# Strassen-Winograd down projection: activations kept as token blocks, loads a pass ahead, the riding tile and one sum made in the gate/up stage

## The chip, the cores and the metric

The kernel runs on one core of one Trainium2 chip. A core has a matrix engine (TensorE, in the profile PE, with its weight loads as PEld), a vector engine (DVE), a scalar engine (ACT), a general engine (POOL) and a queue engine that issues most transfers (SP); transfers are carried by 16 DMA engines. The metric is the device time of one execution in microseconds (us).

## The reference, cut to what matters

One layer of a diffusion backbone over 2048 tokens of width 1024: a mixer (Fourier and retention heads), an output projection, then a SwiGLU feed-forward block with an inner width of 2816, both blocks closed by a post-norm.

```python
u  = modulate(layer_norm(x1), shift, scale)          # (2048, 1024)
h  = silu(u @ w_gate) * (u @ w_up)                   # (2048, 2816)
y  = (h @ w_down) * gate
out = layer_norm(ALPHA * x1 + y, ln2_g, ln2_b)       # (2048, 1024)
```

The inputs and the result are float32. The kernel gets near float32 accuracy with three float16 matmuls for each product: high by high, high by low and low by high halves (`mm3`, L151 to L154). The halves are made by ACT (high) and DVE (low).

## The kernel before, in words

The part that the change touches is the feed-forward block. Its three matrix products are made by Strassen-Winograd's scheme with 7 instead of 8 products, named A11, A12, S2, S1, S3, A22 and S4; S1 to S4 are products of sums of quarters. The tokens are cut in two halves (`sb` 0 and 1). A second level of the scheme is used in the down projection alone.

**Gate/up (925 to 1757 us).** A loop over 11 blocks j of the inner width. For each j SP loads raw weights for gate and for up (`w_raws`, L1080, two halves each into the tile `raw`), POOL forms their sums (L964 to L967), ACT and DVE split the seven results into float16 halves (L148, L149) in tiles of a ring of 12 buffers called `ws`, and PE makes 14 products of 12 matmuls with 512 columns (`prod`). The results go to `sg`; POOL adds the quarters (L1247 to L1249, L1255) and `h_out` (L1228) writes each of the seven outer operands to DRAM tiles `h_d`. Beside each j runs `down(i, c)` (L1139): it loads a piece of the down weights, multiplies it by the gate row (L1147), makes the inner sums on POOL (L1160 to L1163 and L1172 to L1175), splits them into a tile `wdo` with two buffers, and SP writes seven of them to DRAM tiles `wd_d` (five at L1168, two at L1157). The last, odd tile of the inner width (j = 10) is kept apart; its weights (`wl`) are made by `down_last`.

**Down, first part (1757 to 2070 us).** Ten passes: five outer products o (A11, A12, S2, S3, A22) times two token halves, each with its own seven inner products. A pass loads four quarters of h and the odd tile (`h_load`), makes the inner sums with POOL (L1394, L1398, and L1382 for the odd tile) and DVE (L1395, L1396), splits each operand into `ho` (ACT L1134, DVE L1135, three buffers), and PE multiplies: 234 matmuls of 256 columns a pass, four products having the odd tile "ride" with them. The copies `p`, `b_` and `c` (L1500 to L1511, L1443) combine the seven results, which DVE adds to 16 `state` tiles. The h tiles have one buffer, so a pass's loads wait until DVE and POOL are done with the pass before; `tc.issue_after(before)` sets where they stand on SP.

**Down, second part (to 2182 us).** The outer products S1 and S4 (`ONE`), as plain products of 512 columns; then the residual, the norm and the output.

What sets the order: a scheduler puts the instructions of each engine in one fixed order ahead of time, and every engine works through its own in that order. A tile with k buffers waits, when asked for the next time, until the use k turns back has ended. The names and lines that matter are `h_out`, `down`, `h_load`, `w_load`, `h_ops` and `outer`.

Of the kernel before, what the change touches and what calls it, by code (L numbers as in the profile page):

```python
# [15 lines left out]
P = 128  # L16
# [63 lines left out]
def layer_kernel(ctx: ExitStack, tc: tile.TileContext, a, out):  # L80
# [860 lines left out]
    ORDER = (A11, A12, S2, S1, S3, A22, S4)  # L941

# [184 lines left out]
    h_d = [[dram_tile([P, HJ, 2, 512], F16, "h") if o in ONE else dram_tile([P, HJ, 512], F32, "h") for o in range(7)] for _ in range(2)]  # L1127
    wd_d = [dram_tile([P, HJ, 2, 2, 256], F16, "wd") if o in ONE else dram_tile([P, HP, 2, 7, 2, P], F16, "wd") for o in range(7)]
# [8 lines left out]
    def down(i, c):  # L1137

        raws = []  # L1139
        for half in range(2):  # L1140
            raw = raw_tile((P, 2, 4, P))
            r0 = (2 * i + HJ * half) * P
# [10 lines left out]
        def op(o, x):  # L1153
            if o in ONE:
                w = mk(cq, [P, 2, 2, 2, P], F16, tag="wdo", bufs=2)
                split(w[:, :, 0], w[:, :, 1], x)
                Q.dma_start(wd_d[o][:, 2 * i : 2 * i + 2, c], w.rearrange("p k s y n -> p k s (y n)"))  # L1157
                return
# [9 lines left out]
            Q.dma_start(wd_d[o][:, i, c], w)  # L1168
# [10 lines left out]
    def down_last():  # L1179

        raws = []
        for half in range(2):
            raw = raw_tile()
            rv = raw.rearrange("p c n -> p (c n)")
            Q.dma_start(rv, wd_in[(HJ - 1 + HJ * half) * P : HJ * (half + 1) * P])
            G.tensor_tensor(rv, rv, gt2, ALU.mult)
            raws.append(raw)
        for o, t in enumerate(right(*raws)):
            if o in ONE:
                for c in range(2):  # L1190
                    dst = wd_d[o][:, HJ - 1, c].rearrange("p s (y n) -> p s y n", y=2)
                    Q.dma_start(dst, t.rearrange("p s (y c n) -> p c s y n", y=2, c=2)[:, c])
# [3 lines left out]
    def w_load(o, q):  # L1196

        if o == 0 and q in (3, 4):
            r = []
            for lo in range(0, HP, 2):  # L1200
                n = min(2, HP - lo)
                t = ws_tile((P, 2, 2, 2, P))
                Q.dma_start(t[:, :n], wd_d[o][:, lo : lo + n, :, q])
                r.extend(t[:, i] for i in range(n))
            return r
        t = mk(d1 if q < 3 else dq, [P, HP, 2, 2, P], F16, tag=f"wd{q}")
        Q.dma_start(t, wd_d[o][:, :, :, q])
        return [t[:, k] for k in range(HP)]

    def h_load(o, sb):  # L1210

        r = {}
        for qd in (0, 2, 3, 1):
            f, e = divmod(qd, 2)
            r[qd] = mk(d1, [P, HP, 256], tag=f"h{qd}")
            ins = Q.dma_start(r[qd], h_d[sb][o][:, e : 2 * HP : 2, f * 256 : (f + 1) * 256]).ins
        last = ws_tile((P, 512), F32)
        Q.dma_start(last, h_d[sb][o][:, HJ - 1])
        return r, last, ins
# [6 lines left out]
    for j in range(HJ):  # L1226
# [3 lines left out]
        def h_out(sb, o, src):  # L1230
            if o in ONE:
                ht = ws_tile() if j == HJ - 1 else mk(cq, [P, 2, 512], F16, tag="ht", bufs=1)
                half_split(ht, src)
                src = ht
            Q.dma_start(h_d[sb][o][:, j], src)
# [25 lines left out]
        for gu, src in enumerate((wg_in, wu_in)):  # L1261
# [12 lines left out]
            def done(sb, quad, src, ps):  # L1274
# [11 lines left out]
                else:  # L1286
                    c = mk(cq, [P, 512], tag="c", bufs=2)
# [29 lines left out]
            def product(o, sb, loose=False):  # L1317
# [12 lines left out]
                elif o == S3:  # L1330
                    keep(sb, "b", prod(w, o, sb, None, d["x"]))
                    done(sb, 3, d["b"], d["z"])
# [12 lines left out]
            elif j == HJ - 1 and gu == 1:  # L1345
                for sb in (0, 1):
                    for o in ORDER:
                        product(o, sb, True)
                    if sb == 0:
# [6 lines left out]
                        w_next.update((q, w_load(0, q)) for q in range(1, 5))  # L1356
# [20 lines left out]
    def h_ops(q, last):  # L1377

        lt = raw_tile((P, 2, 768), F16)
        with tc.high_priority():  # L1380
            half_split(lt[:, :, 0:512], last)
            G.tensor_tensor(last[:, 0:256], last[:, 0:256], last[:, 256:512], ALU.subtract)  # L1382
            half_split(lt[:, :, 512:768], last[:, 0:256])

        def op(src):
            t = mk(d1, [P, 2, HP, 256], F16, tag="ho", bufs=3)
# [3 lines left out]
        s1 = mk(d1, [P, HP, 256], tag="s1")  # L1390
        for i in range(7):
            with tc.high_priority():
                if i == 1:
                    G.tensor_tensor(s1, q[2], q[3], ALU.add)  # L1394
                    V.tensor_tensor(q[2], q[0], q[2], ALU.subtract)  # L1395
                    V.tensor_tensor(q[0], s1, q[0], ALU.subtract)  # L1396
                elif i == 2:
                    G.tensor_tensor(q[1], q[1], q[0], ALU.subtract)  # L1398
                t = op((q[0], q[1], q[0], q[2], q[3], s1, q[1])[i])
# [5 lines left out]
    def residual(sb, f, name, row, hf):  # L1405
        s_ = state(name, sb, f)
        xr = raw_tile((P, 2, 512))
        for i in range(2):
            t = sb * 8 + row * 4 + f * 2 + i
# [204 lines left out]
```

## Time and profile before

| what | value |
| --- | --- |
| time, median of 3 runs | 2194.0 us (2193.85 to 2196.17) |
| the profiled execution: its time, its span | 2195.93 us, 2194.1 us |
| granted TensorE clock over the span | 0.973 |
| PE busy, DVE busy, POOL busy | 94%, 68%, 39% |
| gate/up | 925 to 1757 us |
| ten passes of the down projection | 1757.35 to 2070.2 us |
| plain products, first matmul without inner scheme to last | to 2182.4 us |
| after the last matmul | 11.7 us |

A start in the profile is counted from the start of the span. A row of the timeline gives start and duration; a bracket gives how long the engine was idle before it and what ended that. A row of the groups gives busy us and mean ns of one instruction. "L1135" is the line that issued it, and where a helper issues for many callers, the tile names tell which one it is.

### The profile page before, as it was taken

What the parts mean: (1) busy time and instruction counts of PE and PEld (TensorE: products, weight loads), DVE (VectorE), ACT (ScalarE), POOL (GpSimd) and SP (SyncE); (2) the same over time, 40 slices, a digit from 0 to 9 for tenths busy, and PEclk for the clock granted to TensorE, in tenths of its full rate; (3) what the DMA queues carried; (4) which work ended last, traced back from release to release, by engine and by line L of the source; (5) the groups of instructions that cost most, each with busy time, mean ns of one, the idle gap of its engine ahead of it and who ended that gap; (6) DMA issues with size and microseconds to landing.
All of it is one profiled execution on the core that took longest, in us unless ns stands there. A gap on an engine that the chain in (4) does not pass through costs nothing. (4 is left out here: it accounts for less than half of the span.)

```text
span 2194.1 us, 31196 instructions
## 1 busy us (share of the span) xinstructions
PE 2051.6 (94%) x11678; PEld 1185.6 (54%) x11678; DVE 1487.7 (68%) x2731; ACT 803.5 (37%) x1442; POOL 845.6 (39%) x838
## 2 busy tenths in 40 slices
PE   6987999999999999889999999999999979898997
PEld 4545676567558444434444444444443458776743
DVE  7767584765688677876656665666556278878866
ACT  5634542332223244443343333333433233333222
POOL 3412321221221156656556655665565142222110
PEclk8998999999999999989999999999999989999999
DMA  9502321221142566614343334343434186779543
GB/s 285 175 4 77 106 80 49 78 61 47 55 119 90 194 209 218 207 66 154 126 144 133 118 129 150 126 136 130 139 116 156 55 266 189 214 213 278 200 146 128
DMA packets 308745, 305.20 MB, mean 139 GB/s; under 512 B 14753, under 2 KB 248049, under 8 KB 307441
## 3 DMA queue, kind: packets, MB, share of 16 engines
q1 hardware_dynamic: 301776, 287.08, 40.9%
q10 hardware_dynamic: 6816, 16.12, 2.0%
q8 instruction: 92, 1.51, 0.3%
q14 instruction: 61, 0.49, 0.1%
HBM read 200.25 MB, written 102.90 MB: 138 GB/s over the span
## 5 line engine op out<-in xcount | busy, mean ns | idle before, releaser
L152 PE MATMUL proj<-ws,uhi 128*128 128x512 f16 (+1 forms) x768 | 251.1, 327 | 2.1 <-ACT sg L751 1.0
L154 PE MATMUL proj<-ws,ulo 128*128 128x512 f16 (+1 forms) x768 | 250.8, 327 | 0.0
L153 PE MATMUL proj<-ws,uhi 128*128 128x512 f16 (+1 forms) x768 | 250.7, 326 | 0.0
L153 PEld LDWEIGHTS <-ws 128*128 128x128 f16 x1296 | 128.2, 99 | 175.9 <-issue 26.6
L152 PEld LDWEIGHTS <-ws 128*128 128x128 f16 x1296 | 128.4, 99 | 157.1 <-issue 9.4
L154 PEld LDWEIGHTS <-ws 128*128 128x128 f16 x1296 | 128.0, 99 | 156.4 <-issue 6.7
L149 DVE SCALAR_TENSOR_TENSOR ws<-raw,ws 128x512 f16<-128x512 f32 x186 | 156.1, 855 | 75.3 <-ACT ws L148 74.3
L148 ACT ACTIVATE ws<-raw 128x512 f16<-128x512 f32 x186 | 112.4, 624 | 124.3 <-DMA raw<-in_w_ffn_gate_dram 36.6
L152 PE MATMUL proj<-u2b,ws 128*128 128x512 f16 x340 | 128.8, 383 | 10.3 <-ACT b L1294 6.3
L152 PE MATMUL misc<-u2a,ws 128*128 128x512 f16 x344 | 131.6, 382 | 6.0 <-ACT p L1294 3.8
L153 PE MATMUL misc<-u2a,ws 128*128 128x512 f16 x344 | 131.8, 383 | 0.0
L154 PE MATMUL misc<-u2a,ws 128*128 128x512 f16 x344 | 131.7, 383 | 0.0
L154 PE MATMUL proj<-u2b,ws 128*128 128x512 f16 x340 | 130.2, 383 | 0.0
L153 PE MATMUL proj<-u2b,ws 128*128 128x512 f16 x340 | 130.1, 383 | 0.0
L1134 ACT CAST ho<-h 128x1280 f16<-128x1280 f32 x60 | 75.0, 1258 | 126.3 <-DMA h<-h 29.0
L149 DVE SCALAR_TENSOR_TENSOR wdo<-raw,wdo 128x256 f16<-128x256 f32 (+1 forms) x100 | 63.4, 655 | 84.8 <-ACT wdo L148 83.8
L167 POOL TENSOR_TENSOR rstd<-ve,mhalf 128x1 f32<-128x1 f32 x66 | 38.4, 590 | 200.8 <-DVE ve L165 177.9
L207 DVE SCALAR_TENSOR_TENSOR macc<-raw,sil,macc 128x128 f32<-128x128 f32 x308 | 109.2, 387 | 3.2
L1135 DVE TENSOR_TENSOR ho<-h,ho 128x1280 f16<-128x1280 f32 x60 | 104.2, 1743 | 9.7 <-ACT ho L1134 9.7
L149 DVE SCALAR_TENSOR_TENSOR wdo<-ws,wdo 128x512 f16<-128x512 f32 (+2 forms) x70 | 59.3, 868 | 75.8 <-ACT wdo L148 74.3
L154 PEld LDWEIGHTS <-ho 128*128 128x128 f16 x764 | 76.2, 100 | 51.1 <-DVE ho L1135 34.2
L152 PEld LDWEIGHTS <-uhi 128*128 128x128 f16 x768 | 75.8, 99 | 44.0 <-issue 2.5
(496 smaller groups left out, 5498.6 us busy)
## 6 DMA issues: line engine op xcount, KB each, us to landing
h<-h SPq DMA_DIRECT2D x40, 640.0 KB, 5.4
raw<-in_w_mod_dram SPq DMA_DIRECT2D x44, 512.0 KB, 4.1
wd<-wdo SPq DMA_DIRECT2D x50, 448.0 KB, 2.5
wd<-wd SPq DMA_DIRECT2D x33, 640.0 KB, 8.5
h<-sg SPq DMA_DIRECT2D x66, 256.0 KB, 2.6
raw<-in_w_ffn_gate_dram SPq DMA_DIRECT2D x22, 512.0 KB, 4.7
raw<-in_w_ffn_up_dram SPq DMA_DIRECT2D x22, 512.0 KB, 5.8
h<-hs SPq DMA_DIRECT2D x44, 256.0 KB, 2.0
```

Source lines behind the costliest of these rows:

```text
L148: S.activation(hi, raw, AF.Copy, scale=scale)
L149: V.scalar_tensor_tensor(lo, raw, scale, hi, ALU.mult, ALU.subtract)
L152: T.matmul(o, sh, mh, start=first, stop=False, skip_group_check=onto)
L153: T.matmul(o, sh, ml, start=False, stop=False, skip_group_check=onto)
L154: T.matmul(o, sl, mh, start=False, stop=last, skip_group_check=onto)
L167: pows.append(G.tensor_tensor(rstd, ve, mhalf[:, 0:n], ALU.pow).ins)
L207: V.scalar_tensor_tensor(acc, raw[:, k], sil[:, v, k : k + 1], acc, ALU.mult, ALU.add)
L1134: S.copy(dst[:, 0], src)
L1135: V.tensor_tensor(dst[:, 1], src, dst[:, 0], ALU.subtract)
```

## The change

**In gate/up.** `h_d` of the five outer operands is stored as four blocks of token quarters. The odd tile is now j = 0 instead of j = 10; its float16 halves (512 columns) and those of the difference of its two halves (256 columns) are made in `h_out` at j = 0 and stored in `hl_d`. This takes 20 tiles of the `ws` ring. For every other j a block of 256 columns is written; at the even ones (j = 2 to 10) `h_out` reads the block that was stored at the j before back into a tile `s1` (two buffers), POOL adds, and SP writes the sum in its place: the inner S1 operand. The down weights are written product by product, so a write has pieces of 512 bytes (896 x 256 elements) where it had 3584 (128 x 1792), and a load has 5 KB in one piece for each partition.

**In the down passes.** Two sets of h tiles, one for each token half; the loads of a pass are asked for at the start of the pass before. The weights of a product are loaded right after its last use. The order of the products becomes A11, A12, S2, S1, S3, S4, A22. S2, S3 and A22 are accumulated onto the PSUM bank of A11, S4 onto that of S1, and DVE adds the bank straight to the state after each product (`outer`); the copies `p`, `b_`, `c` go. POOL's sums go; DVE forms three differences a pass instead of two. `ho` gets four buffers. The residual of two of the state rows moves to the plain products (`row_part`), and for one ACT puts it into the bank.

```diff
-    h_d = [[... else dram_tile([P, HJ, 512], F32, "h") for o in range(7)] for _ in range(2)]
+    h_d = [[... else dram_tile([P, 4, HP, 256], F32, "h") for o in range(7)] for _ in range(2)]
+    hl_d = [[None if o in ONE else dram_tile([P, 2, 768], F16, "hl") for o in range(7)] for _ in range(2)]
...
-            Q.dma_start(wd_d[o][:, i, c], w)
+            Q.dma_start(wd_d[o][:, :, i, c], w)
...
+            elif j == 0:
+                ht = ws_tile()
+                half_split(ht, src)
+                Q.dma_start(hl_d[sb][o][:, :, 0:512], ht)
+                d = mk(cq, [P, 256], tag="s1", bufs=2)
+                G.tensor_tensor(d, src[:, 0:256], src[:, 256:512], ALU.subtract)
+                ht = ws_tile((P, 2, 256))
+                half_split(ht, d)
+                Q.dma_start(hl_d[sb][o][:, :, 512:768], ht)
+            else:
+                k, e = divmod(j - 1, 2)
+                Q.dma_start(h_d[sb][o][:, e, k], src[:, 0:256])
+                if e == 0:
+                    Q.dma_start(h_d[sb][o][:, 2, k], src[:, 256:512])
+                else:
+                    Q.dma_start(h_d[sb][o][:, 3, k], src[:, 256:512])
+                    t = mk(cq, [P, 256], tag="s1", bufs=2)
+                    Q.dma_start(t, h_d[sb][o][:, 2, k])
+                    G.tensor_tensor(t, t, src[:, 256:512], ALU.add)
+                    Q.dma_start(h_d[sb][o][:, 2, k], t)
...
-            t = mk(d1, [P, 2, HP, 256], F16, tag="ho", bufs=3)
+            t = mk(d1, [P, 2, HP, 256], F16, tag="ho", bufs=4)
...
-                if i == 1:
-                    G.tensor_tensor(s1, q[2], q[3], ALU.add)
-                    V.tensor_tensor(q[2], q[0], q[2], ALU.subtract)
-                    V.tensor_tensor(q[0], s1, q[0], ALU.subtract)
-                elif i == 2:
-                    G.tensor_tensor(q[1], q[1], q[0], ALU.subtract)
+                if i == S2:
+                    V.tensor_tensor(q[0], q[2], q[0], ALU.subtract)
+                elif i == S3:
+                    V.tensor_tensor(q[2], q[3], q[0], ALU.subtract)
+                elif i == S4:
+                    V.tensor_tensor(q[1], q[1], q[0], ALU.subtract)
...
+        h_next = h_load(*TWO[n])
...
+            onto = x if q in (S2, S3, A22) else z if q == S4 else None
+            ps = bank(ALL_BANKS, (P, 2, 256)) if onto is None else onto
...
+            if sb and o < 4:
+                w_next[q] = w_load(o + 1, q)
```

**POOL, from block j = 0 to block j = 1.** Before, the last two operations of `down(0, 0)` (L1161, L1163) stand there, then the sums of the gate weights of j = 1 (L964 to L967, first four) and those of its up weights:

```order
357 L1161 TENSOR_TENSOR ws_10253<-raw_10191,ws_10253 128x128
358 L964 TENSOR_TENSOR raw_10276<-raw_10276 128x512
359 L1163 TENSOR_TENSOR ws_10253<-raw_10191,ws_10253 128x128
360 L966 TENSOR_TENSOR raw_10276<-raw_10278,raw_10276 128x512
361 L965 TENSOR_TENSOR ws_10280<-raw_10278,raw_10276 128x512
362 L967 TENSOR_TENSOR raw_10278<-raw_10278,ws_10280 128x512
363 L964 TENSOR_TENSOR raw_10506<-raw_10506 128x512
364 L1147 TENSOR_TENSOR raw_10778<-raw_10778,gt_9767 128x512
```

The quarter sums of j = 0 (L1247) come five rows later. Now, in the changed kernel's own line numbers, the quarter sums (L1272 to L1274, L1280) and the differences of the odd tile (L1245) stand first, and `down(0, 0)` begins after them (L1163):

```order
344 L1272 TENSOR_TENSOR hs_10194<-sg_9780 128x512
345 L1273 TENSOR_TENSOR hs_10194<-sg_9780 128x512
346 L1274 TENSOR_TENSOR hs_10194<-hs_10194,sg_9780 128x512
347 L1280 TENSOR_TENSOR sg_9779<-sg_9779,hs_10153 128x512
348 L1245 TENSOR_TENSOR s_2071_10202<-hs_10194 128x256
349 L1245 TENSOR_TENSOR s_2075_10216<-hs_10194 128x256
350 L1280 TENSOR_TENSOR sg_9780<-sg_9780,hs_10194 128x512
351 L1245 TENSOR_TENSOR s_2078_10241<-sg_9779 128x256
352 L1245 TENSOR_TENSOR s_2082_10270<-sg_9780 128x256
353 L1163 TENSOR_TENSOR ws_10291<-raw_10280 128x128
354 L1165 TENSOR_TENSOR ws_10291<-raw_10280 128x128
```

What moved: `h_out` of j = 0, which waits for the results of the last products of up at j = 0, went ahead of `down(0, 0)` and of the sums of the next gate weights, whose first one comes 20 rows below L1163.

**SP at the same place.** Before, one write of h, then the seven writes of `down(0, 0)` with the load of the second half of the gate weights of j = 1 (L1080) among them:

```order
228 L1235 DMA h_1940_9741<-sg_1993_9769 128x512
229 L1168 DMA wd_1968_9755<-wdo_2045_10202 128x1792
230 L1168 DMA wd_1970_9756<-wdo_2047_10215 128x1792
231 L1168 DMA wd_1972_9757<-wdo_2049_10232 128x1792
232 L1168 DMA wd_1974_9758<-wdo_2051_10245 128x1792
233 L1168 DMA wd_1976_9759<-wdo_2053_10258 128x1792
234 L1157 DMA wd_1978_9760<-wdo_2054_10266 128x2x512
235 L1080 DMA raw_2059_10278<-in_w_ffn_gate_dram 128x8x128
```

Now the same eight follow 24 writes of the odd tile and of S1 and S4 of j = 0, of which the last three are shown:

```order
249 L1243 DMA hl_1980_9761<-ws_2081_10266 256x1x512
250 L1238 DMA h_1966_9754<-ht_2084_10276 128x1024
251 L1248 DMA hl_1980_9761<-ws_2083_10272 256x1x256
252 L1171 DMA wd_1988_9765<-wdo_2089_10296 896x1x256
253 L1171 DMA wd_1990_9766<-wdo_2091_10309 896x1x256
254 L1171 DMA wd_1992_9767<-wdo_2093_10326 896x1x256
255 L1171 DMA wd_1994_9768<-wdo_2095_10339 896x1x256
256 L1171 DMA wd_1996_9769<-wdo_2097_10352 896x1x256
257 L1160 DMA wd_1998_9770<-wdo_2098_10360 128x2x512
258 L1081 DMA raw_2103_10372<-in_w_ffn_gate_dram 128x8x128
```

What moved: the load of the second half of the gate weights stands behind everything that block j = 0 writes. On ACT and DVE the split halves of the odd tile likewise stand ahead of those of `wdo`: eleven low halves of 512 columns, seven of 256 and five additions for `sg` stand on DVE between the result of up's A22 (first token half) and the first low half of `wdo` that POOL's sums feed. On PE, 16 matmuls of the gate product A11 of j = 1 that stood between up's products now come after all of them; the order of the rest is the same there.

**SP in the first down pass.** Before, the h quarters of pass (A11, second token half) (L1216, `h0_2822` first) follow the last writes of h:

```order
547 L1235 DMA h_1958_9750<-hs_2796_16157 128x512
548 L1235 DMA h_1964_9753<-ws_2797_16162 128x1024
549 L1235 DMA h_1956_9749<-sg_2714_15603 128x512
550 L1216 DMA h0_2822_16482<-h_1954_9748 128x5x256
551 L1216 DMA h2_2823_16484<-h_1954_9748 128x5x256
```

Now they (L1219, `h0_2834` first) stand behind the last quarter of the pass after it (`h3_2859`, of A12) and behind the last three round trips of the inner S1 sum (read L1258, write L1260):

```order
759 L1219 DMA h3_2859_16823<-h_1942_9742 128x1280
760 L1238 DMA h_1966_9754<-ws_2833_16518 128x1024
761 L1258 DMA s1_2831_16493<-h_1958_9750 128x256
762 L1260 DMA h_1960_9751<-s1_2829_16483 128x256
763 L1561 DMA ws_3035_19401<-wd_1998_9770 128x1024
764 L1258 DMA s1_2832_16514<-h_1956_9749 128x256
765 L1260 DMA h_1958_9750<-s1_2831_16493 128x256
766 L1260 DMA h_1956_9749<-s1_2832_16514 128x256
767 L1219 DMA h0_2834_16527<-h_1954_9748 128x1280
768 L1219 DMA h1_2835_16529<-h_1954_9748 128x1280
```

What moved: loads of two passes ahead and the round trips went in front of the loads of the very next pass. On PE two matmuls of that next pass stand after the products A11, A12, S1 and S2 of the first pass and before its S3, S4 and A22.

More of the change, by code (lines that the diff above doesn't have):

```diff
@@ L941, in layer_kernel @@
     ORDER = (A11, A12, S2, S1, S3, A22, S4)
+    DOWN = (A11, A12, S2, S1, S3, S4, A22)
     def left(q, s, eng):
@@ L1196, in w_load @@
     def w_load(o, q):
-        if o == 0 and q in (3, 4):
+        n_ = DOWN.index(q)
+        if o == 0 and n_ in (3, 4):
             r = []
@@ L1355, in layer_kernel @@
                         wl = wl_load(0)
-                        w_next.update((q, w_load(0, q)) for q in range(1, 5))
+                        w_next.update((q, w_load(0, q)) for q in DOWN[1:5])
             else:
@@ L1451, in outer @@
         else:
-            V.tensor_tensor(st("21"), st("21"), c, ALU.add)
+            V.tensor_tensor(st(into), st(of), ps, ALU.add)
     def block_done(o, sb, f):
-        if o == A12:
-            residual(sb, f, "11", 0, 0)
-            for i in range(2):
-                moments(sb, f, i, "11", 0, 0)
-        elif o == S3:
-            residual(sb, f, "a", 0, 1)
-            residual(sb, f, "22", 1, 1)
-        elif o == A22:
-            residual(sb, f, "21", 1, 0)
-            for i in range(2):
-                moments(sb, f, i, "21", 0, 1)
@@ L1468, in layer_kernel @@
-    for o in range(5):
-        for sb in range(2):
-            if o == 0 and sb == 0:
-                w = w_next
-                hq, last, before = h_next
-                w.update((q, w_load(0, q)) for q in (5, 6))
-            else:
-                with tc.issue_after(before):
-                    if sb == 0:
-                        w = {0: w_load(o, 0)}
-                    hq, last, before = h_load(o, sb)
-                    if sb == 0:
-                        wl = wl_load(o)
-                        w.update((q, w_load(o, q)) for q in range(1, 7))
-            if o == 0 and sb == 1:
+        if o == S3:
+            residual(sb, f, "22", 1, 1, "21")
@@ new lines, in row_part @@
+    def row_part(sb, name, row):
+        for f in range(2):
+            residual(sb, f, name, row, 0)
+            for i in range(2):
+                moments(sb, f, i, name, 0, row)
+    TWO = [(o, sb) for o in range(5) for sb in range(2)]
+    w = w_next
+    for o, sb in TWO:
+        hq, lt = h_next
+        n = TWO.index((o, sb)) + 1
+        if n < len(TWO):
+            h_next = h_load(*TWO[n])
+        if sb == 0:
+            if o == 0:
+                w.update((q, w_load(0, q)) for q in DOWN[5:])
@@ L1520, in layer_kernel @@
+        if sb:
+            w, wl = w_next, wl_next
+    slots = [(d1, f"h{n}", 1) for n in range(4)] + [(d1, "ho", 4)] * 4 + [(dq, f"h{n}", 1) for n in range(4)]
     turns = [0]
```

171 lines of the change are left out of this document (86 added, 85 removed).

## The prediction

> **What bounds the kernel now.** I read the page first, then the stretches of the down projection, then what PE and POOL wait for there, and last the timeline around the places where the order moves. The page's first lines:
>
> ```profile
> span 2194.1 us, 31196 instructions
> PE 2051.6 (94%) x11678; PEld 1185.6 (54%) x11678; DVE 1487.7 (68%) x2731; ACT 803.5 (37%) x1442; POOL 845.6 (39%) x838
> ```
>
> PE is busy 94%, so whatever the change can gain lies in the places where PE stands. Stretches, with us, then busy us of PE, PEld, DVE, ACT and POOL, granted clock, DMA share and GB/s; the first 38 us of the down projection, the rest of its ten passes, the plain products; and 100 us of gate/up:
>
> ```profile
> 1757.35:1795.13 37.78, 23.85 (x178) 17.90 (x177) 35.40 (x26) 12.67 (x15) 21.25 (x9) 0.89 0.98 304
> 1795.13:2070.20 275.07, 248.95 (x2183) 215.66 (x2184) 233.20 (x221) 93.61 (x95) 64.28 (x25) 0.97 0.72 220
> 2070.20:2182.40 112.20, 112.20 (x522) 50.88 (x520) 67.91 (x148) 22.36 (x30) 10.45 (x15) 1.00 0.43 141
> 1450.00:1550.00 100.00, 100.00 (x465) 45.32 (x464) 62.71 (x78) 37.08 (x73) 63.76 (x61) 1.00 0.41 139
> ```
>
> In gate/up and in the plain products PE never stands; it stands in the passes alone. Who waits there, from 1740 to 2060 us (engine, tile, line, releaser: us, times, longest):
>
> ```profile
> POOL s L1394 <- DMA h<-h: 85.3, 8, 16.9
> POOL h L1398 <- DVE ho L1135: 76.3, 9, 13.9
> PEld L154 <- DVE ho L1135: 34.2, 16, 4.5
> ACT ho L1134 <- DMA h<-h: 29.0, 6, 7.5
> ```
>
> It is one chain: h lands late because its one buffer comes free late, POOL's sum waits for h, DVE's difference for POOL, the split for that, PE for the split. One such stop in the timeline:
>
> ```profile
> 1861.28 0.27 PE L154 MATMUL tq<-wd,ho 128*128 128x256 f16 x1
> ...
> 1861.72 0.27 PE L153 MATMUL zt<-wd,ho 128*128 128x256 f16 x1
> 1865.69 0.39 PE L154 MATMUL zt<-wd,ho 128*128 128x256 f16 x1 [3.69 <-DVE ho L1135]
> 1865.87 0.42 PE L152 MATMUL zt<-wd,ho 128*128 128x256 f16 x1
> 1866.09 0.42 PE L153 MATMUL zt<-wd,ho 128*128 128x256 f16 x1
> ```
>
> Matmuls start every 0.11 us (four steps in 0.44), PE stands for 3.7, and then the starts are 0.2 apart, at about half rate.
>
> **The change part by part.** The sum is made against the profiled execution: 2195.93 us, span 2194.1. The median of the runs shown is 1.9 lower, 2194.0; I add the terms to that.
>
> *Passes after the first.* The 2183 matmuls of the second stretch at 0.11 us need 240 us, so of its 275 us 35 are lost, standing or at half rate. This bounds the gain. Is the cover there? DVE has, in a pass, seven splits, three differences and seven additions of a bank:
>
> ```profile
> L1135 DVE TENSOR_TENSOR ho<-h,ho 128x1280 f16<-128x1280 f32 x50 | 86.9, 1742 | 6.8 <-ACT ho L1134 6.8
> L1135 DVE TENSOR_TENSOR ho<-s,ho 128x1280 f16<-128x1280 f32 x8 | 11.9, 1487 | 0.8 <-ACT ho L1134 0.8
> L1395 DVE TENSOR_TENSOR h<-h,h 128x1280 f32<-128x1280 f32 x9 | 13.4, 1487 | 20.3 <-POOL s L1394 20.3
> L1443 DVE TENSOR_TENSOR c<-b,misc 128x512 f32<-128x512 f32 x4 | 2.7, 681 | 1.1 <-PE misc L154 1.1
> ```
>
> That is 10 x 1.49 + 7 x 0.68 = 19.7 us (21.4 if the splits stay at 1.74) against 234 x 0.11 = 25.7 on PE. DVE is no longer the bound, POOL is out, and the loads are asked for a whole pass earlier. I take 31 of the 35; the range is 22 (a few stops stay where DVE's residual and the next pass's splits meet) to 35. Term: **-31**.
>
> *From block j = 0 to j = 1 in gate/up.* This is the largest added term. Rows of before, in time:
>
> ```profile
> 971.43 0.46 POOL L1160 TENSOR_TENSOR ws<-raw 128x128 f32<-128x128 f32 x1 [6.33 <-PE misc L154]
> 975.18 15.92 SPq L1168 DMA_DIRECT2D wd<-wdo  x5
> 992.76 0.62 SPq L1080 DMA_DIRECT2D raw<-in_w_ffn_gate_dram  x1
> 997.52 0.63 ACT L148 ACTIVATE ws<-raw 128x512 f16<-128x512 f32 x1 [2.60 <-DMA raw<-in_w_ffn_gate_dram]
> 1002.64 0.38 PE L152 MATMUL misc<-u2a,ws 128*128 128x512 f16 x1
> 1006.09 0.38 PE L152 MATMUL misc<-u2a,ws 128*128 128x512 f16 x1
> 1015.59 0.38 PE L152 MATMUL tq<-u2b,ws 128*128 128x512 f16 x1
> ```
>
> POOL begins `down(0, 0)` at 971.43; its first write goes out at 975.18, the second half of the gate weights of j = 1 is asked for at 992.76 (17.6 us later), is there at 997.52 (4.8), and PE first uses it at 1015.59 (A12, bank tq): 18 us to spare. In the new order `down(0, 0)` comes behind `h_out` of j = 0, which waits for up's results. PE has the 16 matmuls of the next A11 (3.45 us) behind up now, so up's A22, first half, which ended at 1006.09, ends at about 1002.6, and its addition about 1003.3. From there DVE has 23 operations before the first low half of `wdo`: eleven of 512 columns, seven of 256, five additions. The nearest rows, of the same forms:
>
> ```profile
> L1135 DVE TENSOR_TENSOR ht<-hs,ht 128x512 f16<-128x512 f32 x20 | 27.7, 1384 | 3.2 <-ACT ht L1134 3.0
> L149 DVE SCALAR_TENSOR_TENSOR wdo<-ws,wdo 128x256 f16<-128x256 f32 x10 | 5.6, 556 | 38.5 <-ACT wdo L148 38.5
> L1289 DVE SCALAR_TENSOR_TENSOR sg<-c,sg 128x512 f32<-128x512 f32 x65 | 62.7, 968 | 1.0
> ```
>
> 11 x 1.38 + 7 x 0.56 + 5 x 0.97 = 24 us: the first write of `down(0, 0)` goes out at about 1027. The same 17.6 and 4.8 us later, and 1.3 for the two halves of the split, A12 could start at 1051. PE, which used to start it at 1015.59, stands in two parts (before A11 and after it), together **+35**. From below: POOL has done its sums by then, and the seven writes may go out in 10 us: +27. From above: each write of the ring waits 1 us longer and DVE stands for the tiles: +43. Two stops just behind it, where PE waited for ACT, go, since ACT has long caught up:
>
> ```profile
> 1025.63 0.56 PE L152 MATMUL misc<-u2a,ws 128*128 128x512 f16 x1 [2.11 <-ACT p L1294]
> 1036.09 0.38 PE L152 MATMUL proj<-u2b,ws 128*128 128x512 f16 x1 [0.84 <-ACT a L1294]
> ```
>
> Term: **-3** (0 to -3).
>
> *First down pass.* The odd tile's splits go, so its early stops shrink; but the h quarters of the next pass stand on SP behind a quarter of the pass after it, which waits for the split of A22 and that for S2's `ho` buffer. PE can do 132 matmuls of the pass and 12 of up's S4 (132 x 0.11 + 12 x 0.22 = 17 us, with 4 of early stops to 1778), then stands. The chain from there:
>
> ```profile
> L1134 ACT CAST ho<-h 128x1280 f16<-128x1280 f32 x51 | 63.8, 1258 | 110.6 <-DMA h<-h 23.2 <-PE misc L154 21.5 <-PE s L154 18.0
> h<-h SPq DMA_DIRECT2D x36, 640.0 KB, 4.7
> h<-sg SPq DMA_DIRECT2D x63, 256.0 KB, 2.6
> 1795.13 0.39 PE L154 MATMUL zt<-wd,ho 128*128 128x256 f16 x1 [3.64 <-DVE ho L1135]
> ```
>
> Split of A22 1.26 + 1.49, a write of the S1 round trips 2.6, its last read 2.6, POOL's addition and the issues some 2, the h quarter 4.7, its split 2.75: 17.4, so PE goes on at about 1796 with 132 done. Before, it went on at 1795.13 with 191 done (A11, A12, S2, S1, S3 and 29 of the next pass): 59 x 0.11 = 6.5 and the 1 us between, **+8** (0 to +13, since the round trips may be over before).
>
> *Gate/up otherwise.* A write of `wd` has pieces of 512 bytes now. The nearest rows: writes in 3584-byte pieces, and gate loads whose rows are 512 bytes.
>
> ```profile
> wd<-wdo SPq DMA_DIRECT2D x50, 448.0 KB, 2.5
> raw<-in_w_ffn_gate_dram SPq DMA_DIRECT2D x20, 512.0 KB, 4.5
> 1673.66 0.38 PE L152 MATMUL proj<-u2b,ws 128*128 128x512 f16 x1 [2.91 <-ACT b L1294]
> ```
>
> At the rate of the loads 448 KB take 3.9 us, 1.4 more; through the ring of two that is 4 us more for each j. In the middle blocks 18 us of slack hide it; at j = 9 to 10 PE waits already (2.91 at 1673.66), so it counts once: **+4** (0 to +10). The Trainium skill, "DMA: Bandwidth & Descriptors", section Specifications, says that transfers run at line rate from 512 bytes up; by that this term would be nothing, and the sum 4 us lower. The rows above speak for a price (114 KB per us in short rows against 179), though a load and a write may differ. The S1 round trips: ten reads and ten more writes at each even j, 2.6 us each, two tiles at a time, some 26 of 72 us; a POOL addition behind a read holds what is behind it on POOL, a late tile holds SP. **+2** (0 to +5).
>
> *Plain products and the end.* PE is full there and DVE has 44 of 112 us free; the moved residuals fit. After the last matmul the same chain of work stands as before. 0 (-3 to +3).
>
> Sum: -31 + 35 - 3 + 8 + 4 + 2 = +15, so 2194 + 15 = **2209 us**.
>
> **The rivals.** *The stop at j = 1 is small* (the faster side). With POOL quiet, DVE's operations of 512 columns take 0.68 (as L1443 above) instead of 1.38, those of 256 some 0.4, and 23 of them 11 x 0.68 + 7 x 0.4 + 5 x 0.68 = 14 us; the writes of `down(0, 0)` start at 1017, go out in 10 us, since POOL has everything ready, and A12 starts 6.1 us later, at 1033. The term is +18 and the time 2192; with the first pass also at nothing it is 2184. It decides where the two terms together fall under 20. For it: PE's long stop leaves DMA and DVE free. Against it: the order is fixed, POOL works on the odd tile's differences in just these 24 us, and the 17.6 us of before came through the ring of two that is still there. Chance 0.26.
>
> *The bank becomes the wait.* S2, S3, A22 and S4 may not start before DVE has read the bank they add to. If DVE's addition stands behind a split that itself waits for PE, each of four products a pass waits for 0.7 and more: 36 products after the first pass, some 0.6 us each, 20 us of the 31 are gone again and the time is 2229. Against it: there is a product of 3.3 to 4 us between a bank's reading and its next use, and DVE has 6 us free a pass. Chance 0.12.
>
> *The change doesn't shorten the passes at all*, since transfers bound them (DMA share 0.72, and 0.98 in the first stretch): loads a pass ahead just queue. 2209 + 25 = 2234. Against it: 220 GB/s where the first stretch has 304, and the same bytes. Chance 0.06.
>
> **How the numbers follow.** The forecast has the remaining 0.56; its own range is 2198 to 2220, from the bounds of the first two terms (nine and eight either way, not all at once). To hold 8 in 10 I reach down to 2182 over most of the first rival and up to 2226. A measurement of this kernel tells about 0.2%, 4.4 us, from no change. Faster by more: the first rival where the passes also give their full 35 or the first pass costs nothing, and the forecast's lower edge, 0.25; within: 0.08; slower: 0.67.
>
> **What would show it.** Right: in the changed profile PE stands twice between 1005 and 1055 us, before bank tq of j = 1, with ACT or DVE `ws` as releaser, 35 us in all; POOL's L1163 starts behind the quarter sums; PE stands some 15 us in the first pass; and from then PE is busy over 98% at a clock near 1.0 until the end. The first term is wrong if PE still waits for `ho` in most passes; the second if A12 of j = 1 starts before 1035; the third if no stop over 8 us lies before 1800.

## The result, and the profile after

The changed kernel takes 2248.0 us (median of 4 runs, 2244.1 to 2252.2) against 2193.9 for the kernel before, measured beside it: slower, by a ratio of 1.0245 (1.0225 to 1.0265). The forecast, 2209 with a range from 2182 to 2226, had the sign and not the size.

The first lines of the page after: PE's busy us are those of before (2053.0 and 2051.6), its share fell from 94% to 91%. Nothing was added to PE's work; it stands longer.

```profile
span 2245.4 us, 31485 instructions
PE 2053.0 (91%) x11678; PEld 1184.5 (53%) x11678; DVE 1458.8 (65%) x2697; ACT 804.1 (36%) x1440; POOL 826.9 (37%) x868
```

The stretches (us, then busy us of PE, PEld, DVE, ACT, POOL, granted clock, DMA share, GB/s). Gate/up from 1060 on in the kernel before:

```profile
1060.00:1757.35 697.35, 685.89 (x3150) 309.04 (x3147) 397.27 (x498) 250.96 (x494) 386.38 (x377) 0.99 0.38 128
```

The same after, then the first 42 us of the down projection, the rest of the ten passes and the plain products:

```profile
1060.00:1835.66 775.66, 731.81 (x3322) 326.35 (x3321) 434.40 (x534) 271.44 (x535) 459.21 (x457) 0.99 0.46 139
1835.66:1877.50 41.84, 21.56 (x144) 15.61 (x144) 23.02 (x19) 11.09 (x13) 13.10 (x9) 0.77 0.84 306
1877.50:2120.90 243.40, 243.19 (x2209) 217.00 (x2210) 183.63 (x163) 80.89 (x69) 0.00 (x0) 0.99 0.70 238
2120.90:2234.30 113.40, 113.40 (x528) 51.47 (x526) 75.45 (x157) 27.05 (x38) 12.12 (x15) 1.00 0.48 159
```

The third line after is what the change was made for: PE is busy in 243.19 of 243.40 us, where before it was in 248.95 of 275.07. The first line after is what undoes it: in gate/up from 1060 on PE now stands for 44 us (775.66 less 731.81), where it had stood for 11, and that is without the two long stops, which lie earlier.

Followed along the trace, the two profiled executions part as follows (span 2194.1 to 2245.4, +51.3):

| point in the trace | before | after | later by |
| --- | --- | --- | --- |
| A12 of the gate weights, block j = 1 (bank tq) | 1015.59 | 1058.84 | 43.3 |
| last matmul of gate/up | 1764.27 | 1844.35 | 80.1 |
| last matmul of the ten passes | 2070.10 | 2120.90 | 50.8 |
| last matmul | 2182.44 | 2234.33 | 51.9 |

Of the 43.3, 3.9 were there before the end of up at j = 0: up's last matmul starts 0.4 later, at 1014.05, and the 16 matmuls of A11 (3.45 us), which stood ahead of it before, are still to come. Why up itself runs later was not followed. So: 39.4 at the start of block 1, 36.8 in the rest of gate/up, 29.3 back in the passes.

What PE waits for from 1000 to 1835 us (engine, bank, line, releaser: us, times, longest): the two stops that the prediction spoke of, and below them many small ones behind ACT's copies `b` and `p`, which in the kernel before came to 8.3 and 4.9 us.

```profile
PE proj L152 <- ACT ws L148: 26.2, 1, 26.2
PE proj L152 <- ACT b L1319: 16.7, 10, 4.5
PE tq L152 <- ACT ws L148: 10.1, 1, 10.1
PE misc L152 <- ACT b L1319: 7.1, 3, 3.8
PE misc L152 <- ACT p L1319: 6.0, 7, 0.9
```

**The start of block 1**, in the timeline: POOL begins `down(0, 0)` (L1163), the five writes start on SP, the second half of the gate weights is asked for (L1081), is there when ACT splits it, and PE makes A12.

```profile
1027.60 0.63 POOL L1163 TENSOR_TENSOR ws<-raw 128x128 f32<-128x128 f32 x1
1033.99 17.71 SPq L1171 DMA_DIRECT2D wd<-wdo  x5
1040.62 0.61 PE L152 MATMUL proj<-u2b,ws 128*128 128x512 f16 x1 [26.19 <-ACT ws L148]
1053.70 0.65 SPq L1081 DMA_DIRECT2D raw<-in_w_ffn_gate_dram  x1
1058.16 0.63 ACT L148 ACTIVATE ws<-raw 128x512 f16<-128x512 f32 x1 [3.02 <-DMA raw<-in_w_ffn_gate_dram]
1058.84 0.61 PE L152 MATMUL tq<-u2b,ws 128*128 128x512 f16 x1 [10.06 <-ACT ws L148]
```

It is the chain of the prediction, link for link: first write, 19.7 us to the load (17.6 said), 4.5 to its landing, then A12. The first write stands 7 us later than the 1027 said: up itself ran 3.9 late, so that DVE's operations ended 3 us late, at 1030.2, and POOL, which only began its sums at 1027.60, made it 4 more. Behind the stops the matmuls take 0.61 to 0.63 instead of 0.38; the granted clock is 0.50 from 1040.62 to 1046.14 and 0.96 in the 2.7 us after that.

**Blocks 2 to 10.** After each block in which the round trips are made, this comes at the start of the next one (here j = 7). The rows in time: SP asks for a stored S1 block back; POOL first does the next `down` (L1150), for which it waited; then the addition; only then may DVE write `sg` again (L1306), ACT use that and copy `a`, and PE go on.

```profile
1533.61 0.38 SPq L1258 DMA_DIRECT2D s<-h  x1
1535.26 1.27 POOL L1150 TENSOR_TENSOR raw<-raw,gt 128x512 f32<-128x512 f32 x1 [3.00 <-DMA raw<-in_w_ffn_down_dram]
1536.49 0.73 POOL L1259 TENSOR_TENSOR s<-s,sg 128x256 f32<-128x256 f32 x1
1537.25 0.69 DVE L1306 TENSOR_TENSOR sg<-p,tq 128x512 f32<-128x512 f32 x1 [4.44 <-POOL s L1259]
1537.97 0.63 ACT L1307 ACTIVATE sg<-sg 128x512 f32<-128x512 f32 x1 [0.76 <-DVE sg L1306]
1538.50 0.57 ACT L1319 COPY a<-proj 128x512 f32<-128x512 f32 x1
1539.12 0.38 PE L152 MATMUL proj<-u2b,ws 128*128 128x512 f16 x1 [1.89 <-ACT a L1319]
```

`sg` holds the result that POOL's addition reads, so the next block's first result has to wait until that addition has run. What holds the addition is either of two things: its read, which by estimate, with the 2.6 us that such reads take in this trace (the median), lands at about 1536.2, and L1150 ahead of it, which waits 3.00 us for a load of its own and is done at 1536.53. No run separates them. DVE and ACT then stay late for the rest of the block, and PE stops again and again behind their copies.

**First pass.** PE stands for 15.4 us. The rows in time: the read back of an S1 block on SP, POOL's addition that waits for it (7 us after the read was asked for), ACT's first copy to a `state` tile, which goes right behind that addition, and PE, whose bank that copy had to read first. The last row is a second stop, behind the split of the next pass's h.

```profile
1860.82 0.44 SPq L1258 DMA_DIRECT2D s<-h  x1
1867.85 0.72 POOL L1259 TENSOR_TENSOR s<-s,hs 128x256 f32<-128x256 f32 x1 [1.91 <-DMA s<-h]
1868.61 0.58 ACT L1469 COPY state<-proj 128x512 f32<-128x512 f32 x1 [10.28 <-POOL s L1259]
1869.24 0.37 PE L152 MATMUL proj<-wd,ho 128*128 128x256 f16 x1 [15.39 <-ACT state L1469]
1877.62 0.28 PE L152 MATMUL s<-wd,ho 128*128 128x256 f16 x1 [3.43 <-ACT ho L1137]
```

### The profile page after: what moved, and what is told of

Its sections match the earlier page's. It is cut to its first block, busy times and chain, and to the rows that moved or that the text cites. A ratio compares the mean times of both kernels' runs of the same rounds, so it can differ in the third digit from the quotient of the medians.

```text
span 2245.4 us, 31485 instructions
## 1 busy us (share of the span) xinstructions
PE 2053.0 (91%) x11678; PEld 1184.5 (53%) x11678; DVE 1458.8 (65%) x2697; ACT 804.1 (36%) x1440; POOL 826.9 (37%) x868
## 4 chain that ended last, share of the span: by engine, by line
PE 39%; DVE 23%; DMA 15%; POOL 13%; ACT 5%; issue 4%; SPq 2%; POOLq 0%; DVEq 0%; ACTq 0%
PE proj L152 6%; PE proj L154 6%; PE proj L153 6%; DVE macc L207 3%; DVE ws L149 3%; DMA raw<-in_w_ffn_down_dram 2%; DMA wd<-wdo 2%; DMA raw<-in_w_ffn_gate_dram 2%; DVE wdo L149 2%; PE s L152 2%; PE s L153 2%; PE s L154 2%; PE misc L153 2%; PE misc L152 2%; DVE sg L1314 2%
## 5 line engine op out<-in xcount | busy, mean ns | idle before, releaser
L152 PE MATMUL proj<-u2b,ws 128*128 128x512 f16 x340 | 131.4, 388 | 53.8 <-ACT ws L148 26.2
L1137 ACT CAST ho<-h 128x1280 f16<-128x1280 f32 x70 | 87.6, 1258 | 175.1 <-DVE h L1415 39.4
L154 PE MATMUL proj<-u2b,ws 128*128 128x512 f16 x340 | 132.2, 389 | 0.0
L153 PE MATMUL proj<-u2b,ws 128*128 128x512 f16 x340 | 132.1, 389 | 0.0
L152 PEld LDWEIGHTS <-uhi 128*128 128x128 f16 x768 | 75.7, 99 | 43.9 <-issue 2.2
L153 PEld LDWEIGHTS <-uhi 128*128 128x128 f16 x768 | 75.4, 98 | 44.1 <-issue 2.6
L154 PEld LDWEIGHTS <-ulo 128*128 128x128 f16 x768 | 75.4, 98 | 42.9 <-issue 0.2
```

The lines of the kernel that those rows point to most:

```text
L152: T.matmul(o, sh, mh, start=first, stop=False, skip_group_check=onto)
L153: T.matmul(o, sh, ml, start=False, stop=False, skip_group_check=onto)
L154: T.matmul(o, sl, mh, start=False, stop=last, skip_group_check=onto)
L1137: S.copy(dst[:, 0], src)
```

## The experiments

The theory was that two causes cost the time, each by itself: the odd tile's work at j = 0, which puts `down(0, 0)` and the next weights behind it, and the S1 round trips, which hold `sg`. Rivals: the small pieces of the writes of `wd`; SP, on whose queue the round trips stand; and passes that only look better because something else moved. All ratios are to the kernel before, measured beside the run; "no addition" and "down first, sum in the passes" ran on another chip than the rest of the experiments. Stages are from the profiled execution: the last matmul of gate/up, and the ten passes from the first matmul of the down projection to the last of 256 columns. Each is one execution: the kernel before and the one with the new `wd` alone have equal times, and their passes differ by 5 us, so smaller differences in these columns say little.

| kernel | median us | ratio (95%) | gate/up ends | ten passes |
| --- | --- | --- | --- | --- |
| before | 2193.9 | 1 | 1764.3 | 312.8 |
| changed kernel | 2248.0 | 1.0245 (1.0225 to 1.0265) | 1844.4 | 285.2 |
| sum made in the passes | 2193.4 | 1.0008 (0.9999 to 1.0018) | 1800.5 | 276.8 |
| odd tile raw | 2207.7 | 1.0074 (1.0056 to 1.0091) | 1799.8 | 288.8 |
| both | 2153.6 | 0.9834 (0.9819 to 0.9848) | 1760.5 | 274.0 |
| down(0, 0) first | 2217.4 | 1.0125 (1.0110 to 1.0140) | 1817.8 | 286.4 |
| down first, sum in the passes | 2170.4 | 0.9904 (0.9886 to 0.9922) | 1775.2 | 275.8 |
| no read back | 2210.0 | 1.0093 (1.0077 to 1.0109) | 1816.2 | 278.7 |
| no addition | 2206.7 | 1.0079 (1.0064 to 1.0094) | 1819.6 | 270.2 |
| round trips on POOL's queue | 2248.3 | 1.0275 (1.0256 to 1.0294) | 1842.7 | 284.7 |
| before, with the new `wd` alone | 2189.6 | 0.9998 (0.9990 to 1.0007) | 1763.2 | 307.6 |
| both, one set of h tiles | 2170.4 | 0.9913 (0.9898 to 0.9928) | 1761.2 | 295.1 |

### The S1 sum made in the passes again

```diff
-                    t = mk(cq, [P, 256], tag="s1", bufs=2)
-                    Q.dma_start(t, h_d[sb][o][:, 2, k])
-                    G.tensor_tensor(t, t, src[:, 256:512], ALU.add)
-                    Q.dma_start(h_d[sb][o][:, 2, k], t)
...
+                if i == A11:
+                    G.tensor_tensor(q[2], q[2], q[3], ALU.add)
```

> The inner S1 sum goes back to POOL in the down passes (one addition of 1280 columns a pass), so the even blocks read nothing back and write no sum; the rest is the changed kernel. Theory 1 (the round trips hold SP's queue in the odd blocks, and what stands behind them comes late): the stops of blocks 2 to 10 fall back to those of before, some 30 us less, and the first down pass loses its 15 us stop: 2248 becomes 2205 to 2218, and the passes stay without a stop, since the addition is hidden by loads that are a pass ahead. Theory 2 (the 512-byte pieces of the weight writes make gate/up slow): 2248 less the first pass's 15, so 2230 to 2240, and the stops of the odd blocks stay.

2193.4 us, more gained than either theory had. Gate/up ends 43.9 earlier than in the changed kernel, 2 of them there before A12 of block 1 starts; from there to the end of gate/up it takes 743.7 us instead of 785.5. The passes take 8.4 less, and the stop behind `state` is gone. The two stops at block 1 are still there (26.2 and 9.8). What PE waits for from 1060 to 1760:

```profile
PE proj L152 <- ACT b L1315: 7.5, 3, 4.6
PE misc L152 <- ACT b L1315: 3.3, 2, 2.5
PE misc L152 <- ACT p L1315: 1.4, 2, 0.8
```

12.2 us, where the changed kernel has 40.2 in the same window and the kernel before 12.5.

### The odd tile stored raw and split in the down projection again

```diff
-                ht = ws_tile()
-                half_split(ht, src)
-                Q.dma_start(hl_d[sb][o][:, :, 0:512], ht)
...
+                Q.dma_start(hl_d[sb][o], src)
...
```

The splits and POOL's difference of the odd tile stand in `h_ops` of each pass again.

> The odd tile stays at j = 0 but is stored as it comes, in float32, and split in the down passes as before; the S1 round trips stay. Theory 1 (the 20 ws tiles of the split halves put the down weights of j = 0 and the next gate weights behind up's results): the two stops between 1010 and 1060 us go, 36 to 40 us less, 2208 to 2214. Rival (the halves cost engine time wherever they are made): what is gained at j = 1 comes back in the passes, where DVE then has 21 us of 25.6, at over 10 us: 2220 or more.

2207.7 us, just under what was expected. A12 of block 1 starts at 1017.5, and no stop is over 2.4 us there: without the odd tile's work in front the two stops do not come. The passes take 3.6 more than in the changed kernel, but with the sum also in the passes the raw tile makes them 2.8 shorter, so neither shows a price of its splits there.

### Both edits

> Both edits: S1's inner sum on POOL in the down passes, the odd tile stored in float32. Theory 1: the two gains add, 2248 - 40 - 35 = 2173, within 2162 to 2182, clearly faster than the kernel before (2194), since nothing but the passes' gain of some 30 us is left. Theory 2 (short pieces of the weight writes): 2190 to 2205.

2153.6 us: 1.7% faster than the kernel before, and faster than expected. Gate/up from 1060 and the passes after the first:

```profile
1060.00:1753.53 693.53, 684.26 (x3158) 309.17 (x3157) 402.07 (x500) 253.12 (x495) 392.10 (x377) 1.00 0.42 130
1790.00:2027.57 237.57, 237.57 (x2174) 212.56 (x2173) 202.96 (x177) 85.96 (x81) 37.07 (x15) 1.00 0.70 242
```

Gate/up ends about where it did before (1760.5 and 1764.3), and in the passes after the first PE never stands, though POOL works 37.07 us there. The four medians of one chip add up: before 2191.5; both edits 37.8 below it; the odd tile's work alone 39.8 above that (2193.4); the round trips alone 54.1 above it (2207.7). -37.8 + 39.8 + 54.1 = +56.1, and the change, measured apart from these four, is at +54.1. To some 2 us the two causes do not overlap, and together they are the whole loss.

### `down(0, 0)` ahead of up's products at j = 0

```diff
+            if j == 0 and gu == 1:
+                down(0, 0)
...
-        if j < 2 * HP:
+        if 0 < j < 2 * HP:
```

> The changed kernel with one call moved: the down weights of j = 0 are asked for ahead of up's products instead of behind them, so that their tiles of the ring come before those of the odd tile. No work is added or left out. Theory 1 (it is the place, not the work): the 36 us of the two stops shrink to under 8 us: 2208 to 2220. Rival (ACT's, DVE's and POOL's work for the odd tile itself makes the gate weights late): at most 15 us less, 2233 or more.

2217.4 us, within what theory 1 expected, but the stops did not shrink to under 8 us: one of 14.2 is left. The last of the odd tile's splits on ACT, the first split of the waiting weights, and PE:

```profile
1025.31 0.41 ACT L1137 CAST ws<-s 128x256 f16<-128x256 f32 x1
1025.62 1.15 ACT L148 ACTIVATE ws<-raw 128x512 f16<-128x512 f32 x2
1026.30 0.61 PE L152 MATMUL proj<-u2b,ws 128*128 128x512 f16 x1 [14.23 <-ACT ws L148]
```

The weights are there, but their split stands on ACT behind the last split of the odd tile. So the load behind `down(0, 0)`'s writes makes the larger part of the loss, and the splits standing in front make the rest. The same edit together with the sum in the passes:

> The changed kernel with the down weights of j = 0 asked for ahead of up's products and with S1's inner sum on POOL in the down passes: the odd tile's halves stay in gate/up. Theory 1 (place of the down weights and round trips are the two costs, independent of each other): 2248 - 31 - 55 = 2162, within 2155 to 2170, a little slower than with the tile stored in float32 (2153.6). Rival (the odd tile's halves in gate/up save work in the passes that the other version pays): 2150 or less.

2170.4 us, just over the upper edge. The stop is again 14.2. By the ratios the kernel is 15 us above that of both edits, by the medians 19; and of the first pair, the edit took 28 of the 40. So of the 40 us at block 1 some 12 to 19 are the odd tile's own work in front of the weights' splits, and the rest, the larger part, is the place of `down(0, 0)`. Giving the odd tile tiles outside the `ws` ring was not tried.

### The round trips taken apart

Without the read back (POOL adds the two halves of the tile at hand):

```diff
-                    Q.dma_start(t, h_d[sb][o][:, 2, k])
-                    G.tensor_tensor(t, t, src[:, 256:512], ALU.add)
+                    G.tensor_tensor(t, src[:, 0:256], src[:, 256:512], ALU.add)
```

> The changed kernel without the reading back: POOL adds the two halves of the block at hand instead, so the inner S1 operand is another sum (left out: the true S1 sum), while POOL's addition, both writes and the tile s1 stay. Theory 1a (the read is what holds SP: it waits for the write of the block that it reads and for a free s1 tile, and its 2 us stand before each addition): 2248 less 25 or more, under 2223, near the kernel without round trips (2193). Theory 1b (the number of instructions on SP and the second write weigh): less than 12 us gained, 2236 or more.

Without the addition (what was read is written again):

```diff
-                    G.tensor_tensor(t, t, src[:, 256:512], ALU.add)
```

> The changed kernel with the round trips kept (read, tile s1, second write), but without POOL's addition between them (left out: the inner S1 sum, the block goes back as it was read). Theory A (POOL stands: the addition waits for the read, and the sums of the next weights stand behind it): as fast as without the read, 2205 to 2218. Theory B (SP stands: the read waits for a write and a free tile, the second write waits for the read, and other transfers stand behind them): 2235 or more.

2210.0 and 2206.7 us: 20 and 17 above the kernel before on their chips, where the change is 54 above it: either half taken away gives 34 to 37 us of the 52 that both give. Both times are where theory 1a and theory A had them, but not for their reasons. The next section is about SP; and PE's waits are behind ACT's copies, not behind the sums of the next weights.

From A12 of block 1 to the end of gate/up, 785.5 us in the changed kernel and 743.7 with both halves taken away, the two take 761.0 and 762.8. A read without an addition or an addition without a read thus still costs 17 to 19 there, and what these are was not followed. The other 23 to 25 need both: an addition that comes late while it holds `sg`. Without the read, the order puts the last additions of a block right behind POOL's quarter sums or close to it, and DVE hardly waits for them. DVE's waits from 1060 to 1760, first of the changed kernel, then without the read back (where lines stand one lower):

```profile
DVE sg L1306 <- POOL s L1259: 23.7, 8, 4.7
```

```profile
DVE sg L1305 <- POOL s L1258: 5.0, 4, 1.3
```

The first pass points the same way. PE's stop behind ACT's copy to `state` is 15.4 us in the changed kernel and 14.0 with the raw odd tile, where both halves are there; with the addition alone, and with the read alone:

```profile
1829.10 0.37 PE L152 MATMUL proj<-wd,ho 128*128 128x256 f16 x1 [3.95 <-ACT state L1468]
```

```profile
1835.29 0.37 PE L152 MATMUL proj<-wd,ho 128*128 128x256 f16 x1 [6.59 <-ACT state L1468]
```

With neither it is absent. Why `state` waits for POOL at all is read from the code, not shown by a run: its tiles lie in space that the gate/up stage frees only when its last tiles, the round trips' among them, are done.

### The round trips on another queue

```diff
-                    Q.dma_start(t, h_d[sb][o][:, 2, k])
+                    G.dma_start(t, h_d[sb][o][:, 2, k])
...
-                    Q.dma_start(h_d[sb][o][:, 2, k], t)
+                    G.dma_start(h_d[sb][o][:, 2, k], t)
```

> The changed kernel with the read and the second write of the round trips issued by POOL instead of SP; no work is left out. Theory 1 (SP's fixed order: loads and writes behind a waiting round trip come late): gate/up loses most of its stops in the odd blocks, 15 to 40 us less, 2208 to 2233. Rival (the round trips hold POOL, whose addition waits for the read, and with it the sums of the next weights): no gain or a loss, 2243 or more.

2248.3 us, ratio 1.0275 (1.0256 to 1.0294): nothing gained. In the changed kernel SP waits in these places (1060 to 1760):

```profile
SPq L1258 <- DMA h<-s: 28.8, 20, 3.4
SPq L1258 <- DMA h<-sg: 16.0, 9, 2.6
SPq L1260 <- POOL s L1259: 14.8, 19, 1.7
```

With SP freed of them, POOL waits instead, ahead of its own work:

```profile
POOL s L1258 <- DMA h<-sg: 10.9, 4, 7.8
POOL s L1258 <- DMA h<-s: 10.1, 6, 3.9
```

SP's 60 us of waiting look like the cause, but the run without the addition speaks against it: SP waits 66 us at the read and the second write there, and gate/up is 23 us shorter all the same. On either of the two queues that were tried an engine in fixed order has to wait for the round trip. One thing stays open: DVE's wait for POOL at `sg`, 23.7 us in the changed kernel, is only 2.9 here, and nothing is gained by it. With POOL issuing the round trips the time goes elsewhere, and where was not followed.

### The layout of the down weights alone, in the kernel before

```diff
-    wd_d = [... else dram_tile([P, HP, 2, 7, 2, P], F16, "wd") for o in range(7)]
+    wd_d = [... else dram_tile([P, 7, HP, 2, 2, P], F16, "wd") for o in range(7)]
...
-            Q.dma_start(wd_d[o][:, i, c], w)
+            Q.dma_start(wd_d[o][:, :, i, c], w)
```

> The kernel before with one thing of the change: the layout of the down weights (writes in 512-byte pieces, loads of 5 KB in one piece). Theory 1 (the S1 round trips slow the odd blocks, not these pieces): no more than 0.2% from before, the five writes of a block take 16 us as before. Theory 2 (short pieces cost a price in gate/up): 4 to 25 us slower.

Ratio 0.9998 (0.9990 to 1.0007): in the kernel's time the pieces of 512 bytes cost nothing. The five writes at a middle block, of the kernel before and of this run, take the same time through the ring:

```profile
1183.64 15.97 SPq L1168 DMA_DIRECT2D wd<-wdo  x5
```

```profile
1185.61 16.00 SPq L1168 DMA_DIRECT2D wd<-wdo  x5
```

But a single write is slower. Over gate/up (925 to 1757), where the kernel before has 2.5 us from issue to landing, this run has 3.5:

```profile
wd<-wdo SPq DMA_DIRECT2D x50, 448.0 KB, 3.5
```

ACT waits longer for tiles of the ring (54.0 us against 33.5 from 1060 to 1757), and this wait is hidden, since PE does not wait for `wdo`. Whether it is the size of the pieces or their new places in DRAM is not separated; the edit changes both.

### Both edits, with one set of h tiles

```diff
-            r.append(mk(dq if sb else d1, [P, HP, 256], tag=f"h{n}"))
+            r.append(mk(d1, [P, HP, 256], tag=f"h{n}"))
...
```

The tiles of the second set also leave the list `slots`, from which the plain products take theirs.

> The kernel with both edits (2153.6) with one set of h tiles for both token halves, as before the change, so that a pass's quarters are loaded when the pass before has done with them. Theory 1 (the second set, which lets the loads run a pass ahead, is what removed the stops of the passes): they come back, 15 to 35 us more, 2168 to 2188. Rival (less DVE work and no chain of POOL sums removed them): 2154 to 2160.

2170.4 us, as theory 1 had it: ratio 0.9913 (0.9898 to 0.9928), 0.0079 above that of the two sets, 17 us of loss for one set. The passes after the first:

```profile
1790.00:2049.30 259.30, 242.93 (x2177) 212.81 (x2175) 187.99 (x176) 84.55 (x81) 45.33 (x16) 0.99 0.63 218
```

PE is out for 16 us. In the passes, 38.7 us were gained by both edits over the kernel before; without the second set 21 of them are lost. The rest, with some 5 us of uncertainty, is left to the other changes there (one buffer more for `ho`, banks added straight to the states, the products' order) and was not divided further.

## Why the prediction was off

The terms, predicted and measured, in the order of the trace (sum of the right column: the span's +51.3):

| term | predicted | measured |
| --- | --- | --- |
| up to the end of up at j = 0 | 0 | +3.9 |
| from there to A12 of block j = 1 | +35 | +39.4 |
| rest of gate/up: S1 round trips (+2), two small stops (-3) | -1 | +36.8 |
| `wd` in pieces of 512 bytes (by its own run) | +4 | 0 |
| first pass | +8 | +5.7 |
| passes after the first | -31 | -35 |
| plain products and the end | 0 | +0.5 |

**Passes after the first: right.** DVE's splits and sums fit, POOL's wait for h is gone, and of the 35 lost us 0.2 are left. The rival of the bank that has to be read first did not come: DVE waits for PE at the additions (L1471, in the last section), not PE for DVE. The rival of transfers as the bound is out too: they ran at 238 GB/s, where they had run at 220. One part of the change was not needed for it: with POOL's sum back in the passes PE is still busy in 237.57 of 237.57 us. The price of the last rival was added up wrong, too: without the term of -31 the time is 2240, not 2234.

**Block 0 to block 1: right in mechanism, 4 short,** and within its bounds (27 to 43). The failed step is "POOL has done its sums by then", which stood in the lower bound, and which the middle value used as well by starting the first write right behind DVE's 23 operations. When those had ended, the first split of `down(0, 0)` had to wait for POOL, 4 us more. The first rival, a small stop, is wrong: PE stood for 26.2 and 10.1.

**The round trips: the term that failed.** The step was "a POOL addition behind a read holds what is behind it on POOL, a late tile holds SP", set at +2 (0 to +5). No row is given for that price; the slack that the prediction names for the middle blocks is 18 us, that of the weights' loads. By the pairs of runs with and without them, from A12 of block 1 to the end of gate/up, the round trips cost 39 to 44 us (782.3 less 743.0 with the raw tile, 785.5 less 743.7 in the changed kernel, 789.8 less 745.3 with `down(0, 0)` first). The step left out what the addition itself holds: `sg`, the tile that it reads. By the runs without one half this makes 23 to 25 of the 42 in the changed kernel; the cause of the other 17 to 19 stays open. The rows that would have shown the hold on `sg` stood in the trace of before, POOL's last two operations on `sg` in a block and DVE's first two writes to it in the next:

```profile
1461.91 1.72 POOL L1255 TENSOR_TENSOR sg<-sg,hs 128x512 f32<-128x512 f32 x1
1464.91 1.27 POOL L1255 TENSOR_TENSOR sg<-sg,hs 128x512 f32<-128x512 f32 x1 [1.28 <-issue]
```

```profile
1467.26 0.68 DVE L1281 TENSOR_TENSOR sg<-p,tq 128x512 f32<-128x512 f32 x1
1472.44 0.68 DVE L1281 TENSOR_TENSOR sg<-p,zt 128x512 f32<-128x512 f32 x1
```

First to first and second to second, that is 4 to 6 us of slack, not 18. In the changed kernel at j = 7 the additions end some 9 us after those operations on POOL (the first at 1537.22, with L1280 done at 1528.33). Had the term been set at 39 to 44, the sum would have been +52 to +57. Nor was gate/up as full as said: "In gate/up and in the plain products PE never stands" was read from 100 us of it, and from 1060 to 1757 PE stood for 11.

**First pass: right in size, wrong in place,** so the size is luck. The stop was to come behind the loads on SP's queue, after S2. It came behind POOL's last additions, at S2's accumulation on the bank of A11, through the tile `state`. The prediction's chain from there (the h quarters behind SP's order) is the second, smaller stop of 3.4 us.

**The pieces of 512 bytes: a price, but hidden.** A write takes 1.0 us longer, from 2.5 to 3.5, where 1.4 was said. What failed is "through the ring of two that is 4 us more": the five writes take 16.0 us as before, and the kernel's time does not change. The Trainium skill, "DMA: Bandwidth & Descriptors", section Specifications, has line rate from 512 bytes up; by that the term is zero. The ratio of 0.9998 (0.9990 to 1.0007) agrees, the single write does not.

## What to carry to other kernels

Before a step with a wait is added to a stage in which the matrix engine is always busy, list every tile that the step reads and ask who writes that tile next: the wait is priced against the time to that write, not against the slack of some load that stands nearby. An addition that reads back from DRAM what was stored one block earlier holds its other operand until the read has landed and whatever stands ahead of it on its engine is done; here it was cheaper, by 54 us, where both operands are loaded anyway. A transfer that gets slower costs nothing while its wait stays off the matrix engine's path: look at the transfer and at the kernel's time separately. And work that is pulled from a bound stage into one that is full has to be timed by itself: here the passes gained 39 us without either of the two moves into gate/up, and the moves cost 40 and 54.

## What the runs showed that was not expected

DVE's 1280-column splits are faster when POOL is silent. In the passes, the groups on DVE (busy us, mean ns; then the idle time before them and its releaser) of the changed kernel, and of the kernel with both edits, where POOL has its sum:

```profile
L1138 DVE TENSOR_TENSOR ho<-h,ho 128x1280 f16<-128x1280 f32 x63 | 94.0, 1491 | 34.5 <-ACT ho L1137 34.3
L1471 DVE TENSOR_TENSOR state<-state,proj 128x512 f32<-128x512 f32 x16 | 10.9, 683 | 7.5 <-PE proj L154 7.5
```

```profile
L1138 DVE TENSOR_TENSOR ho<-h,ho 128x1280 f16<-128x1280 f32 x62 | 107.1, 1728 | 16.0 <-ACT ho L1137 15.6
```

1491 ns against 1728, 16% more, while POOL is busy for only 37 of 238 us. It is not that each split is a little slower: in the kernel with both edits, of the 60 that the trace lists singly, the 53 that no POOL operation overlaps take 1.47 to 1.49 us, and the 7 that one overlaps take 3.3 to 4.2. One of these:

```profile
1818.46 3.57 POOL L1407 TENSOR_TENSOR h<-h,h 128x1280 f32<-128x1280 f32 x1 [12.79 <-DMA h<-h]
1820.08 3.29 DVE L1138 TENSOR_TENSOR ho<-h,ho 128x1280 f16<-128x1280 f32 x1 [0.21 <-ACT ho L1137]
```

The split ends 1.3 us after POOL's operation. The Trainium skill, "SBUF — State Buffer", section "SBUF: two separate sides", says that a DVE operation with two SBUF inputs and a POOL operation that reads SBUF take a shared pair of ports in turn, each for its whole length; these rows agree with that. It cost nothing here: PE was busy throughout in both.
